# Root mean square norms in a two-layer token mixer: scaled squares, one vector step ahead of the root, and half of the gating beside it

## The chip, the cores and the metric

The kernel runs on one core of a Trainium2 chip. The metric is the device time of one execution in microseconds, the median over several runs. The engines are named as in the profile: PE is TensorE (PEld is its weight load), DVE is VectorE, ACT is ScalarE, POOL is GpSimd and SP is SyncE, which issues most transfers.

## The reference

Two layers, 256 latent and 256 context tokens of width 1024. In each layer the tokens go through a mixer (one wide projection, a two-way RG-LRU branch and a two-way HGRN2 branch, both projected, gated and merged) and through a convolutional SwiGLU FFN. What the change touches are the norms around them:

```python
def rms_norm(x, g):
    x32 = x.astype(jnp.float32)
    y = x32 * lax.rsqrt(jnp.mean(x32 * x32, axis=-1, keepdims=True) + EPS)
    return (y * g.astype(jnp.float32)).astype(x.dtype)
...
        hl = rms_norm(xl, g_pre_mix[l]) * (1.0 + ml[1]) + ml[0]
...
        xl = xl + ml[2] * rms_norm(yl, g_post_mix[l])
        hl = rms_norm(xl, g_pre_ffn[l]) * (1.0 + ml[4]) + ml[3]
```

A mixer or FFN output is normalised, multiplied by a gate row (which holds the post-norm's gain too) and added to the stream; the stream is normalised again, scaled and shifted for the next projection.

## The kernel before

All products run on PE in 32-bit floats, split in two: an operand x becomes a high part (a rounding copy on ACT, `whi` at L236 for weights) and a low part (a subtraction on DVE, `wlo` at L237), and `mm3` issues three matmuls for one product (L242 to L244). Weights come in pieces of one megabyte (`raw`), each cut into two pieces of 128x1024; in the first pieces behind a stage boundary (`self.fine`) a piece is cut into four quarters of 128x256. Feature products (`feat_group`) hold weights as the stationary side and move 512 tokens in layer 0 and 256 in most of layer 1; so layer 1 and a few groups of layer 0 consist of 256-column matmuls.

The output projections (`tok_product`, L495) put tokens on partitions: two rows of 128 tokens, each in two PSUM banks of 512 columns. `post` (L465) takes them over, row by row. ACT squares each half and accumulates its sum (L473, two columns of `ss`). DVE multiplies each half with the gate row (`yg`, L474). `rstd` (L399) adds the two sums (L402), then calls `rpow` (L405), which scales by 1/width and adds EPS (L408) and has POOL raise the result to -1/2 (L410). DVE adds `yg` times the root to the stream row `xt` (L477), in two halves. If a norm follows, `norm_row` (L414) squares `xt` on ACT (L419), takes its root by the same `rstd`, and scales it on DVE into `xh` (L422). After both rows, `norm_cols` (L430) transposes `xh` on PE (L436), applies scale and shift on ACT (L441) and DVE (L443), and forms the low part (L445); these tiles are the moving side of the next products.

`post` runs six times: layer-0 mixer for context and latent, layer-0 FFN for both, layer-1 mixer and layer-1 FFN for the latent tokens; the last one has no norm behind it and writes the output. `norm_rows` does four more rows at the start. So `rstd` runs 12 + 10 + 4 = 26 times; `rpow` is also called 16 times by the HGRN2 heads (L975).

The order of each engine's instructions is settled at compile time by a scheduler that goes by priority and by its own estimate of when operands are ready; `post` runs under `high_priority`. So weight subtractions for the next stage can stand between the steps of a norm on DVE. An order edge without a semaphore (`add_manual_dep` with NoSync) fixes which of two instructions on one engine comes first. `act` (L92) uses it to keep the activations with tables in program order. Small tiles come from the pool `sm`, four buffers for each tag; `rstd` uses the tag `ms` and `rpow` the tags `m1` and `r1` for one column.

Of the kernel before, what the change touches and what calls it, by code (L numbers as in the profile page):

```python
# [8 lines left out]
F32 = mybir.dt.float32  # L9
F32R = mybir.dt.float32r  # L10
U8 = mybir.dt.int32
AF = mybir.ActivationFunctionType
ALU = mybir.AluOpType

P = 128
D = 1024
# [5 lines left out]
EPS = 1e-6  # L22
# [29 lines left out]
class Net:  # L52
# [36 lines left out]
        return self.ax.tile([P, 512], F32, tag="ax", name=self.nm("ax"))  # L89


    def act(self, **kw):  # L92
        ins = self.nc.scalar.activation(**kw)  # L93
        if self.last is not None:
            self.tc.add_manual_dep(ins.ins if hasattr(ins, "ins") else ins, self.last, mybir.DependencyInfo(
                mybir.DependencyClass.NoSync, mybir.DependencyReason.DATA), reason="table order")
        self.last = (ins.ins if hasattr(ins, "ins") else ins).name
        return ins


# [295 lines left out]
                            for j in range(4)])  # L396


    def rstd(self, ss, width):  # L399
        nc = self.nc  # L400
        ms = self.sm.tile([P, 1], F32, tag="ms", name=self.nm("ms"))
        nc.vector.tensor_tensor(out=ms, in0=ss[:, 0:1], in1=ss[:, 1:2], op=ALU.add)  # L402
        return self.rpow(ms, 1, width)

    def rpow(self, ss, n, width):  # L405
        nc = self.nc
# [7 lines left out]
    def norm_row(self, xt, x):  # L414
        nc = self.nc
        ss = self.sm.tile([P, 2], F32, tag="ss2", name=self.nm("ss"))
        halves = [slice(0, 512), slice(512, D)]
        for j, sl in enumerate(halves):
            nc.scalar.activation(out=x[:, sl], in_=xt[:, sl], func=AF.Square, accum_out=ss[:, j:j + 1])  # L419
        rs = self.rstd(ss, D)  # L420
        for sl in halves:
            nc.vector.tensor_scalar(out=x[:, sl], in0=xt[:, sl], scalar1=rs, scalar2=None, op0=ALU.mult)  # L422

# [41 lines left out]
    def post(self, pool, pss, st, gate, xts, xdst, norm=None):  # L465
        nc = self.nc
        xh = [pool.tile([P, D], F32, tag="xh", name=self.nm("xh"), bufs=2) for _ in xts]
        cols = [slice(0, 512), slice(512, D)]
        for i, (halves, xt, x) in enumerate(zip(pss, xts, xh)):
            ss = self.sm.tile([P, 2], F32, tag="ss2", name=self.nm("ss"))  # L470
            yg = pool.tile([P, D], F32, tag="yg", name=self.nm("yg"), bufs=2)
            for j, (ps, sl) in enumerate(zip(halves, cols)):
                nc.scalar.activation(out=x[:, sl], in_=ps, func=AF.Square, accum_out=ss[:, j:j + 1])  # L473
                nc.vector.tensor_tensor(out=yg[:, sl], in0=ps, in1=gate[:, sl], op=ALU.mult)  # L474
            rs = self.rstd(ss, D)
            for sl in cols:
                nc.vector.scalar_tensor_tensor(out=xt[:, sl], in0=yg[:, sl], scalar=rs, in1=xt[:, sl],  # L477
                                               op0=ALU.mult, op1=ALU.add)
                if not norm:
                    nc.sync.dma_start(out=xdst[2 * st + i][:, sl], in_=xt[:, sl])  # L480
            if norm:
                nc.sync.dma_start(out=xdst[2 * st + i], in_=xt)
                self.norm_row(xt, x)
        if norm:
            a, s, h, psum = norm
            for k2 in range(KD // 2):
                self.norm_cols(pool, xh, a, s, st, h, k2, psum)
# [7 lines left out]
    def tok_product(self, w, nk, act, psum):  # L495
        nc = self.nc
        pss = [[psum() for _ in range(2)] for _ in range(2)]
        pcs = {}

        def step(i, k):  # L500
            hi, lo = pcs[k]
            ah, al = act(k, i)
            for n in range(2):
                out = pss[i][n]
                nc.tensor.matmul(out=out, lhsT=ah, rhs=hi[:, n, :], start=k == 0, stop=False)  # L505
                nc.tensor.matmul(out=out, lhsT=ah, rhs=lo[:, n, :], start=False, stop=False)  # L506
            for n in range(2):
                nc.tensor.matmul(out=pss[i][n], lhsT=al, rhs=hi[:, n, :], start=False, stop=k == nk - 1)  # L508

        for k0 in range(0, nk, 2):  # L510
            raw = self.raw()
            r3 = raw.rearrange("p (k n) -> p k n", k=2)
            nc.sync.dma_start(out=r3, in_=w[k0 * P:(k0 + 2) * P, :].rearrange("(k p) n -> p k n", p=P))
            for kk in range(2):
                pcs[k0 + kk] = self.piece(r3[:, kk, :].rearrange("p (a b) -> p a b", a=2), (2, 512))
            ks = [k for k in (k0, k0 + 1) if k < nk - 3]
            for i in range(2):
                for k in ks:
                    step(i, k)
        for i in range(2):  # L520
            for k in range(nk - 3, nk):
                step(i, k)
        return pss
# [750 lines left out]
```

## Time and profile before

| | us |
|---|---|
| median of three runs | 1762.72 |
| lowest, highest run | 1760.85, 1768.89 |
| the profiled execution | 1772.73 |
| its span, first to last instruction | 1771.0 |

The profile is of one execution. Its page gives the busy time of each engine over the span; lists by line give count and duration of each kind of instruction; the timeline gives single instructions with the idle time of the engine ahead of them in brackets, and who ended it. A mean over the whole span says little of the norms, since they run in six short stages; these are read from the timeline and from windows.

### The profile page before, as it was taken

Reading aid. Unit: us, or ns where it says so; the run is one execution under the profiler, and the core shown is the slowest. Engines: PE = TensorE matmul, PEld = TensorE weight load, DVE = VectorE, ACT = ScalarE, POOL = GpSimd, SP = SyncE. Lnnn points to the kernel's source line nnn. Section 1 sums busy time; section 2 is a strip of 40 time slices with the busy share of each in tenths; the row PEclk is TensorE's granted clock in tenths of the full one; section 3 lists DMA queues with packets and bytes.
Section 4 is the critical chain, followed back from the end, with each engine's and each line's share of the span. In section 5 each row is a group of like instructions: output and inputs, shape, how many; then the busy total and the mean of one; then the engine's idle time right before and its main releaser. Section 6 shows DMA issues by size and latency. Waiting matters only on the chain.

```text
span 1771.0 us, 30585 instructions
## 1 busy us (share of the span) xinstructions
PE 1695.1 (96%) x12279; PEld 1421.9 (80%) x12279; DVE 1271.5 (72%) x2313; ACT 903.4 (51%) x1567; POOL 39.9 (2%) x65
## 2 busy tenths in 40 slices
PE   6999999999999999999999999999989999979998
PEld 3777887888888877878878877788987778979996
DVE  3688777788687787987676476777558776767754
ACT  3886823344443446533333355887435554555543
POOL 1000000000000000000000000000000000000000
PEclk9999999999999999999999999999999999989999
DMA  9422377333333376455454674333773424555563
GB/s 295 133 84 84 113 224 230 121 117 100 97 122 99 124 250 257 137 189 170 148 188 143 198 260 165 104 109 109 240 238 115 135 85 132 199 169 182 183 221 119
DMA packets 235289, 282.91 MB, mean 160 GB/s; under 512 B 18156, under 2 KB 211324, under 8 KB 235148
## 3 DMA queue, kind: packets, MB, share of 16 engines
q1 hardware_dynamic: 232156, 271.35, 46.7%
q10 hardware_dynamic: 2880, 9.51, 1.5%
q8 instruction: 96, 1.57, 0.4%
q14 instruction: 45, 0.37, 0.1%
q0 software_dynamic: 112, 0.11, 0.0%
HBM read 263.09 MB, written 17.85 MB: 159 GB/s over the span
## 4 chain that ended last, share of the span: by engine, by line
PE 66%; DVE 16%; DMA 7%; ACT 7%; issue 3%; POOL 1%; SPq 1%; DVEq 0%; POOLq 0%; ACTq 0%
PE mm L242 15%; PE mm L243 15%; PE mm L244 15%; DVE wlo L237 4%; PE mm L506 3%; PE mm L505 3%; PE mm L508 3%; DVE acc L307 2%; DMA raw<-in_w_ada_dram 2%; ACT whi L236 2%; DMA dm<-sb 1%; PE ax L850 1%; ACT r L93 1%; PE ax L506 1%; PE ax L508 1%
## 5 line engine op out<-in xcount | busy, mean ns | idle before, releaser
L242 PE MATMUL mm<-hi,whi 128*128 128x512 f32 (+1 forms) x1792 | 621.4, 348 | 3.6 <-DVE sb L697 2.3
L243 PE MATMUL mm<-lo,whi 128*128 128x512 f32 (+1 forms) x1792 | 618.6, 345 | 4.9 <-DVE lo L445 4.8
L244 PE MATMUL mm<-hi,wlo 128*128 128x512 f32 (+1 forms) x1792 | 616.4, 344 | 2.0 <-DVE wlo L237 1.9
L237 DVE TENSOR_TENSOR wlo<-raw,whi 128x1024 fp32r<-128x1024 f32 (+1 forms) x408 | 436.3, 1080 | 250.8 <-ACT whi L236 237.6
L236 ACT ACTIVATE whi<-raw 128x1024 fp32r<-128x1024 f32 (+1 forms) x408 | 378.6, 943 | 435.6 <-PE mm L243 229.3
L242 PEld LDWEIGHTS mm<-hi,whi 128*128 128x128 f32 x1792 | 339.5, 190 | 50.2 <-issue 4.3
L243 PEld LDWEIGHTS mm<-lo,whi 128*128 128x128 f32 x1792 | 339.0, 189 | 46.3 <-DVE lo L445 6.2
L244 PEld LDWEIGHTS mm<-hi,wlo 128*128 128x128 f32 x1792 | 338.2, 189 | 42.9 <-DVE wlo L237 3.2
L307 DVE SCALAR_TENSOR_TENSOR acc<-raw,s,acc 128x256 f32<-128x256 f32 x448 | 194.4, 478 | 2.6
L865 DVE TENSOR_TENSOR QK<-QK,T 128x512 f32<-128x512 f32 (+1 forms) x84 | 101.5, 1219 | 8.5 <-PE ax L850 5.2
L242 PE MATMUL mm<-whi,hi 128*128 128x256 f32 x256 | 72.9, 285 | 1.0 <-ACT whi L236 0.9
L243 PE MATMUL mm<-wlo,hi 128*128 128x256 f32 x256 | 72.1, 282 | 1.5 <-DVE wlo L237 1.5
L244 PE MATMUL mm<-whi,lo 128*128 128x256 f32 x256 | 71.9, 281 | 0.0
L874 ACT ACTIVATE kt<-QK 128x256 f32<-128x256 f32 (+1 forms) x60 | 40.8, 689 | 58.3 <-DVE QK L865 35.8
L505 PE MATMUL mm<-whi,fh 128*128 128x512 f32 x176 | 68.6, 390 | 0.0
L506 PE MATMUL mm<-wlo,fh 128*128 128x512 f32 x176 | 68.5, 389 | 0.0
L410 POOL TENSOR_TENSOR rs<-ms,mhalf 128x1 f32<-128x1 f32 (+2 forms) x42 | 29.7, 706 | 1549.3 <-DVE ms L408 1549.3
L93 ACT ACTIVATE acc<-acc 128x512 f32<-128x512 f32 (+1 forms) x44 | 22.6, 516 | 69.1 <-DVE acc L1081 64.3
L508 PE MATMUL mm<-whi,fl 128*128 128x512 f32 x176 | 54.2, 389 | 0.0
L242 PEld LDWEIGHTS mm<-whi,hi 128*128 128x128 f32 x256 | 48.9, 191 | 2.9 <-ACT whi L236 1.1
L243 PEld LDWEIGHTS mm<-wlo,hi 128*128 128x128 f32 x256 | 49.0, 191 | 2.2 <-DVE wlo L237 2.2
L244 PEld LDWEIGHTS mm<-whi,lo 128*128 128x128 f32 x256 | 48.9, 191 | 0.0
(225 smaller groups left out, 2466.2 us busy)
## 6 DMA issues: line engine op xcount, KB each, us to landing
raw<-in_w_in_dram SPq DMA_DIRECT2D x72, 1024.0 KB
raw<-in_w_ada_dram SPq DMA_DIRECT2D x48, 1024.0 KB
raw<-in_ffn_w_up_dram SPq DMA_DIRECT2D x44, 1024.0 KB
raw<-in_ffn_w_down_dram SPq DMA_DIRECT2D x33, 1024.0 KB
raw<-in_w_out_dram SPq DMA_DIRECT2D x12, 1024.0 KB
raw<-in_w_proj_rg_dram SPq DMA_DIRECT2D x8, 1024.0 KB
raw<-in_w_proj_hg_dram SPq DMA_DIRECT2D x8, 1024.0 KB
xs<-xt SPq DMA_DIRECT2D x10, 512.0 KB
```

Source lines behind the costliest of these rows:

```text
L93: ins = self.nc.scalar.activation(**kw)
L236: nc.scalar.activation(out=v(hi)[:, part, :], in_=src[:, part, :], func=AF.Copy)
L237: nc.vector.tensor_tensor(out=v(lo)[:, part, :], in0=src[:, part, :], in1=v(hi)[:, part, :], op=ALU.subtract)
L242: nc.tensor.matmul(out=out, lhsT=L[0], rhs=R[0], start=start, stop=False)
L243: nc.tensor.matmul(out=out, lhsT=L[0], rhs=R[1], start=False, stop=False)
L244: nc.tensor.matmul(out=out, lhsT=L[1], rhs=R[0], start=False, stop=stop)
L307: nc.vector.scalar_tensor_tensor(out=acc[:, st, :], in0=r3[:, k, :], scalar=s, in1=acc[:, st, :], op0=ALU.mult, op1=ALU.add)
L505: nc.tensor.matmul(out=out, lhsT=ah, rhs=hi[:, n, :], start=k == 0, stop=False)
L506: nc.tensor.matmul(out=out, lhsT=ah, rhs=lo[:, n, :], start=False, stop=False)
L508: nc.tensor.matmul(out=pss[i][n], lhsT=al, rhs=hi[:, n, :], start=False, stop=k == nk - 1)
L865: nc.vector.tensor_tensor(out=u, in0=u, in1=sub(t, 1, [[-1, 2], [2, W2 // B], [0, B]]), op=ALU.mult)
L874: nc.scalar.activation(out=kt.rearrange("p (n h j) -> p n h j", h=2, j=B), in_=sub(qk, W2, [[2 * B, W2 // (2 * B)], [W2 + B, 2], [1, B]]), ...
```

## The change

The squares carry a scale of 1/sqrt(1024) (`ROOT`), so that the accumulated sums of the two halves are means already. `rstd` then takes one DVE step, which adds the two columns and EPS, in place of the addition and the scale-and-add, and calls POOL itself; the buffer tag `m1` is no longer used. In `post` the gate product of the second half is put behind that step by an order edge, so that DVE does it while POOL takes the root. The helper `behind` makes the edge, and `act` now uses it too, with the same effect as before.

```diff
+    def behind(self, ins, first):
+        self.tc.add_manual_dep(getattr(ins, "ins", ins), getattr(first, "ins", first).name, mybir.DependencyInfo(
+            mybir.DependencyClass.NoSync, mybir.DependencyReason.DATA), reason="order")
...
         if self.last is not None:
-            self.tc.add_manual_dep(ins.ins if hasattr(ins, "ins") else ins, self.last, mybir.DependencyInfo(
-                mybir.DependencyClass.NoSync, mybir.DependencyReason.DATA), reason="table order")
-        self.last = (ins.ins if hasattr(ins, "ins") else ins).name
+            self.behind(ins, self.last)
+        self.last = ins
...
-    def rstd(self, ss, width):
+    def rstd(self, ss):
         nc = self.nc
         ms = self.sm.tile([P, 1], F32, tag="ms", name=self.nm("ms"))
-        nc.vector.tensor_tensor(out=ms, in0=ss[:, 0:1], in1=ss[:, 1:2], op=ALU.add)
-        return self.rpow(ms, 1, width)
+        first = nc.vector.tensor_scalar(out=ms, in0=ss[:, 0:1], scalar1=ss[:, 1:2], scalar2=EPS, op0=ALU.add, op1=ALU.add)
+        rs = self.sm.tile([P, 1], F32, tag="r1", name=self.nm("rs"))
+        nc.gpsimd.tensor_tensor(out=rs, in0=ms, in1=self.mhalf[:, 0:1], op=ALU.pow)
+        return rs, first
+
+
+    ROOT = D ** -0.5
...
-            nc.scalar.activation(out=x[:, sl], in_=xt[:, sl], func=AF.Square, accum_out=ss[:, j:j + 1])
-        rs = self.rstd(ss, D)
+            nc.scalar.activation(out=x[:, sl], in_=xt[:, sl], func=AF.Square, scale=self.ROOT, accum_out=ss[:, j:j + 1])
+        rs, _ = self.rstd(ss)
...
             for j, (ps, sl) in enumerate(zip(halves, cols)):
-                nc.scalar.activation(out=x[:, sl], in_=ps, func=AF.Square, accum_out=ss[:, j:j + 1])
-                nc.vector.tensor_tensor(out=yg[:, sl], in0=ps, in1=gate[:, sl], op=ALU.mult)
-            rs = self.rstd(ss, D)
+                nc.scalar.activation(out=x[:, sl], in_=ps, func=AF.Square, scale=self.ROOT, accum_out=ss[:, j:j + 1])
+            nc.vector.tensor_tensor(out=yg[:, cols[0]], in0=halves[0], in1=gate[:, cols[0]], op=ALU.mult)
+            rs, first = self.rstd(ss)
+
+            self.behind(nc.vector.tensor_tensor(out=yg[:, cols[1]], in0=halves[1], in1=gate[:, cols[1]], op=ALU.mult), first)
```

## Rows read from the trace of the kernel before

**Rows 1.** The page, first part: busy us (share of the span) and instructions.

```profile
PE 1695.1 (96%) x12279; PEld 1421.9 (80%) x12279; DVE 1271.5 (72%) x2313; ACT 903.4 (51%) x1567; POOL 39.9 (2%) x65
```

**Rows 2.** Lists of L402, L408, L410: count, ns min/median/max, first and last start.

```profile
L402 DVE TENSOR_TENSOR ms<-ss x26: 144/151/160, 7.4 to 1765.0; 128x1 f32<-128x1 f32 x26
...
L408 DVE TENSOR_SCALAR ms<-ms x26: 139/148/155, 7.6 to 1765.2; 128x1 f32<-128x1 f32 x26
...
L410 POOL TENSOR_TENSOR rs<-ms,mhalf x42: 548/596/1394, 7.9 to 1765.5; 128x1 f32<-128x1 f32 x26, 128x4 f32<-128x4 f32 x8, 128x2 f32<-128x2 f32 x8
```

**Rows 3.** Timeline of PE in the post-norm stages: start, us, engine, line [idle <-releaser].

```profile
691.39 1.53 PE L436 MATMUL mm<-ident,xh 128*128 128x128 f32 x12 [0.58 <-DVE xh L422]
...
713.55 0.38 PE L244 MATMUL mm<-hi,wlo 128*128 128x256 f32 x1 [1.40 <-DVE wlo L237]
...
1048.25 1.53 PE L436 MATMUL mm<-ident,xh 128*128 128x128 f32 x12 [0.57 <-DVE xh L422]
...
1096.20 1.53 PE L436 MATMUL ax<-ident,xh 128*128 128x128 f32 x12 [1.51 <-DVE xh L422]
...
1567.31 1.05 PE L436 MATMUL ax<-ident,xh 128*128 128x128 f32 x4 [3.83 <-DVE xh L422]
1572.89 2.82 PE L436 MATMUL ax<-ident,xh 128*128 128x128 f32 x12 [4.53 <-DVE xh L422]
```

**Rows 4.** Timeline of the tail, behind the last matmul.

```profile
1763.84 1.29 DVE L474 TENSOR_TENSOR yg<-mm,gt 128x512 f32<-128x512 f32 x2 [0.39 <-ACT xh L473]
1764.19 0.20 ACT L473 ACTIVATION_READ_ACCUMULATOR xh<-mm 128x1 f32 x1
1765.05 0.15 DVE L402 TENSOR_TENSOR ms<-ss 128x1 f32<-128x1 f32 x1
1765.23 0.15 DVE L408 TENSOR_SCALAR ms<-ms 128x1 f32<-128x1 f32 x1
1765.53 0.55 POOL L410 TENSOR_TENSOR rs<-ms,mhalf 128x1 f32<-128x1 f32 x1 [3.53 <-DVE ms L408]
```

**Rows 5.** List by line and shape, Sigmoid with scale -1 and without: us, mean ns.

```profile
L93 ACT ACTIVATE QK<-mm 128x512 f32<-128x512 f32 x16 | 9.6, 600 | 0.0
...
L93 ACT ACTIVATE T<-mm 128x512 f32<-128x512 f32 x16 | 9.5, 596 | 0.0
```

**Rows 6.** Timeline of DVE, layer-1 mixer: two pairs of the norm's steps.

```profile
1565.46 0.15 DVE L402 TENSOR_TENSOR ms<-ss 128x1 f32<-128x1 f32 x1
...
1565.86 0.15 DVE L408 TENSOR_SCALAR ms<-ms 128x1 f32<-128x1 f32 x1
...
1567.48 0.15 DVE L402 TENSOR_TENSOR ms<-ss 128x1 f32<-128x1 f32 x1
...
1567.88 0.14 DVE L408 TENSOR_SCALAR ms<-ms 128x1 f32<-128x1 f32 x1
```

**Rows 7.** Timeline, layer-0 FFN, context: a power and a weight subtraction.

```profile
1042.30 1.21 DVE L237 TENSOR_TENSOR wlo<-raw,whi 128x1024 fp32r<-128x1024 f32 x1
...
1042.52 1.39 POOL L410 TENSOR_TENSOR rs<-ms,mhalf 128x1 f32<-128x1 f32 x1 [2.93 <-DVE ms L408]
```

**Rows 8.** Timeline, layer-0 mixer, context: a power and a gate half.

```profile
683.10 0.68 DVE L474 TENSOR_TENSOR yg<-mm,gt 128x512 f32<-128x512 f32 x1
...
683.27 0.56 POOL L410 TENSOR_TENSOR rs<-ms,mhalf 128x1 f32<-128x1 f32 x1 [4.53 <-DVE ms L408]
```

**Rows 9.** Windows: PE, PEld, DVE, ACT, POOL busy, granted clock, DMA share, GB/s.

```profile
1563.00:1568.00 5.00, 1.17 (x7) 0.56 (x5) 4.93 (x16) 4.32 (x14) 0.56 (x1) 0.96 0.26 105
...
1576.00:1581.00 5.00, 4.42 (x21) 4.13 (x21) 4.86 (x10) 2.07 (x5) 0.00 (x0) 0.50 0.00 0
```

**Rows 10.** Windows of PE alone (256-column matmuls only): busy (count), clock, DMA, GB/s.

```profile
1255.00:1302.00 47.00, 47.00 (x417) 1.00 0.73 236
...
sum 128.00, PE 128.00; mean PE 14.22
...
1591.00:1703.00 112.00, 112.00 (x953) 1.00 0.58 188
```

## The prediction, made before the result was known

> **What bounds the kernel now.** I read the page's busy shares first: PE is busy for 1695.1 of 1771.0 us [rows 1], so TensorE sets the time, and a norm counts only where PE waits for it. Three lists by line then show how often the touched steps run: 26 additions of two half sums, 26 scale-and-add steps (L408 has 16 more in the HGRN2 heads, which stay), 26 powers on POOL among 42, each step near 0.15 us on DVE and the power near 0.6 us [rows 2]. Next I listed PE's waits in the stages where a post-norm runs; the reader is to see the bracket at the end of each row, the idle time and who ended it. Six waits end on the norm chain or on DVE work queued behind it [rows 3]: 0.58 us (layer-0 mixer, context), 1.40 (layer-0 mixer, latent), 0.57 (layer-0 FFN, context), 1.51 (layer-0 FFN, latent), and 3.83 and 4.53 (layer-1 mixer, where PE has nothing else to do). With the tail after the last matmul, where the chain alone runs [rows 4], that is the whole field: 12.4 us of waits and some 4 us of tail. The four norms at the start of the program wait beside PE's own wait for a weight transfer, so I cost them at nothing; the transfer is the cover.
>
> **The change part by part.**
>
> *Scale in Square.* The instruction count stays; a scale rides in the same ACTIVATE. The nearest rows are Sigmoid with and without a scale, 600 and 596 ns for 128x512 [rows 5]. I take 0; the ends are 0 and +4 ns for each of 52 squares, at most 0.2 us.
>
> *One step in place of two.* The new step adds two columns and a constant on 128x1. No row has this form; the neighbours are 0.151 and 0.148 us at the median [rows 2], so I take 0.15. What goes is one step with its distance. With nothing between, the two start 0.18 us apart [rows 4]. Where the compile-time order has put a quarter of a weight subtraction between them, 0.40 us apart [rows 6]; the second pair there stands for a third like it, 3.6 us later. The subtraction itself is not saved, only the power's wait for it.
>
> *Second gate half under the power.* Where both halves run back to back ahead of the sums, they take 1.29 us together [rows 4]; the second half then leaves the path. In the tail: the last squares' accumulator read starts at 1764.19 and takes 0.20, so it ends at 1764.39; the first gate half ends at about 1764.49 (1763.84 + 1.29/2), so the single step can start at about 1764.5. The power starts 0.30 us after its step now (1765.23 to 1765.53), so at 1764.8 in place of 1765.53: **0.73 us** gained. The ends are 0.55 (0.18 of it left hidden under a late accumulator) and 0.83 (1.29/2 + 0.18).
>
> *The added wait.* The second gate half now stands behind the new step, which waits for ACT's second accumulator. Behind it in DVE's queue stand weight subtractions for the next stage and the residual step. In the tail the accumulator is ready 0.1 us before DVE is, so the wait costs nothing; where ACT is late, DVE loses at most the half that it cannot start, 0.65 us. In the second row of the other stages the gate half already runs beside a power, so only the shorter pair is left to gain.
>
> *Power beside DVE work.* One power took 1.39 us, started 0.22 us into a whole weight subtraction [rows 7]; one beside a gate half took 0.56 [rows 8]. I take 0.56 for the new overlap. The Trainium skill, "SBUF — State Buffer", Who interferes with whom, says that a VectorE instruction with two SBUF inputs blocks a GpSimd instruction that reads SBUF until it is done. The subtraction has two SBUF inputs and the gate half one (the other is PSUM), so the page and both rows agree; its rule speaks against this change only if the gate half counted. Then the power would end about 0.4 us behind the half, as it does behind the subtraction (1042.30 + 1.21 to 1042.52 + 1.39), and the tail's gain would be about 0.43 us.
>
> *The stages with waits.* Layer-1 mixer: three pairs on the chain. In the first, DVE is almost full (4.93 of 5 us [rows 9]), so removing one step gives about 0.1; the other two give 0.4 each, less 0.1 where a subtraction holds the power up. The first row's gate half, 0.65, leaves the path to its residual and to the next squares. Sum 0.1 + 2 x 0.3 + 0.65, some 1.3 us; the low end 0.7 is without that last term, the high end 2.8 lets the order of ACT and DVE close up fully. Layer-0 FFN, latent: the same pattern against a wait of 1.51, so 1.2 (0.4 to 1.5). Layer-0 mixer, latent: there a subtraction stood behind the residual step that waited for the power, so the wait of 1.40 may shrink: 0.8 (0 to 1.4). The two context stages: the last pair is 0.2 apart and the waits are 0.58 and 0.57: 0.4 together (0 to 1.15).
>
> *The clock.* PE restarts after the layer-1 mixer at a granted clock of 0.50, its level of 1.2 GHz, having been busy for 1.17 us only between 1563 and 1568 [rows 9]. PE still idles for several us there, so I count no change; the ends are a restart that is fully fast, a gain of some 2.2 us (half of the 4.42 us for which PE is busy at that level between 1576 and 1581), and no change.
>
> *Sum.* 0.73 + 1.3 + 1.2 + 0.8 + 0.4 = 4.4 us, between 1.7 and 7.7 without the clock. The profiled execution took 1772.73 us (span 1771.0, 1.73 around it) and would take 1768.3. It stands 10 us over the median of the three runs, 1762.72; I take the same 4.4 us off that: **1758.3 us**.
>
> **The rivals.** *A, PE restarts at the quicker pace.* Windows in which PE does nothing but 256-column matmuls at full clock show two paces: 417 in 47 us, 112.7 ns each, and 953 in 112 us, 117.5 ns each [rows 10]. The slow stretch begins with the restart after the layer-1 mixer and holds through the layer-1 FFN, while other stretches hold the quick pace. What sets the pace is not shown; it changes only at interruptions, so a restart moved by a microsecond may fall the other way. Price: 953 x 4.8 ns = 4.6 us, so 1753.7 us. *B, little of it is on the path.* DVE's order could keep subtractions between the step and the power, or ACT could be what ends last, so that beyond the tail only half a microsecond remains: 1.2 us gained, 1761.5 us. The full DVE in [rows 9] speaks for it, the waits in [rows 3] against. Here too belongs that the order edge does nothing: in second rows the gate half is already under a power. *C, slower.* The quick stretches, 128 us in nine windows [rows 10], fall to the slow pace: each of the 1140 or so matmuls (128/0.1127) costs 4.8 ns more, 5.5 us. It could come from the moved restarts, or from memory: the tag for the second step's four buffers is gone, so every tile allocated behind it moves. Since the gain is 4.4 us, C decides from about 920 matmuls on. With the sum at its low end of 1.7 us the time is 1762.7 - 1.7 + 5.5 = 1766.5 us; were the wide matmuls moved too, it could be more, and nothing in the trace prices that. For C: the paces do differ. Against: quick stretches appear after many different interruptions.
>
> **How the numbers follow.** Chances: the forecast 0.46, A 0.24, B 0.16, C 0.14. The forecast's own range is 1755.0 to 1761.0 (the sum between 1.7 and 7.7). The range that should hold it 8 times in 10 runs from 1750 (A with the sum at its high end: 1762.7 - 7.7 - 4.6) to 1767 (C). A measurement of this kernel can tell about 0.5%, 8.8 us, from no change: under 1753.9 is faster, over 1771.5 slower. Faster: somewhat over half of A, 0.14, and of the forecast the end with the clock's gain, 0.11: 0.25. Slower: half of C, 0.07, and 0.02 for mishaps in the order: 0.09. The same: 0.66.
>
> **What would show it.** Right: 26 single steps near 0.15 us and no L402 pair; in the tail, the power starting 0.7 us sooner after the squares, 0.56 us long, with the second gate half beside it; the waits of 3.83 and 4.53 us shorter by about 1.3 together; 1.51, 1.40 and 0.37 shorter. Wrong: powers of 1 us and more in the post-norms; PE's waits unchanged, with subtractions between step and power; a layer-1 FFN at 112.7 ns for each narrow matmul (A), or quick stretches at 117.5 (C).

## The result, and the profile after

The changed kernel took 1775.76 us (median of six runs, 1773.09 to 1779.67) beside 1765.81 us for the kernel before (six runs, 1759.3 to 1769.25): a ratio of 1.0067, 95% interval 1.0044 to 1.0090. By the ratio it is slower by some 12 us (the two medians stand 10 us apart), where 4.4 us less had been forecast, and it lies outside the forecast's range of 1755.0 to 1761.0 and the wider one that ended at 1767. The profiled execution took 1775.03 us. Its mean granted clock was 0.995, beside 0.991 in the profiled execution of the kernel before, so a lower clock is not what made it slower.

The first line of the page after answers to [rows 1]: PE is busy for 1705.4 us in place of 1695.1, with the same 12279 matmuls, while DVE has 26 instructions fewer, as planned.

```profile
span 1773.3 us, 30552 instructions
...
PE 1705.4 (96%) x12279; PEld 1419.6 (80%) x12279; DVE 1270.7 (72%) x2287; ACT 903.2 (51%) x1567; POOL 38.9 (2%) x65
```

So the added time is busy time of an engine that the change does not touch. The list of PE by line and shape says which matmuls: first the kernel before, then the one after (columns: shapes, count | busy us, mean ns | idle before).

```profile
L242 PE MATMUL mm<-hi,whi 128*128 128x512 f32 x992 | 395.2, 400 | 3.3 <-DVE sb L697 2.3 <-ACT whi L236 0.9
L243 PE MATMUL mm<-lo,whi 128*128 128x512 f32 x992 | 392.6, 396 | 1.6 <-DVE lo L445 1.6
L244 PE MATMUL mm<-hi,wlo 128*128 128x512 f32 x992 | 391.5, 395 | 0.5 <-DVE wlo L237 0.5
...
L505 PE MATMUL mm<-whi,fh 128*128 128x512 f32 x176 | 68.6, 390 | 0.0
```

```profile
L246 PE MATMUL mm<-hi,whi 128*128 128x512 f32 x992 | 399.5, 404 | 3.0 <-DVE sb L708 2.5 <-ACT whi L240 0.5
L247 PE MATMUL mm<-lo,whi 128*128 128x512 f32 x992 | 396.8, 400 | 1.5 <-DVE lo L454 1.5
L248 PE MATMUL mm<-hi,wlo 128*128 128x512 f32 x992 | 396.4, 400 | 0.0
...
L516 PE MATMUL mm<-whi,fh 128*128 128x512 f32 x176 | 68.6, 390 | 0.0
```

The reader is to see two things. The wide (512-column) feature products became 4, 4 and 5 ns longer on the mean, which is 992 x 13 ns = 12.9 us; the token products, of the same size and just as many columns (L505 before, L516 after), did not. Windows in which PE does nothing but one kind of wide product say the same as a pace. In each kernel the first window holds feature products of layer 0, the second token products of the layer-0 FFN, the third the 256-column products of the layer-1 FFN (columns: window, its length, PE busy and count, granted clock, DMA share, GB/s; the third window of before stands in [rows 10]).

Before:

```profile
177.00:237.00 60.00, 60.00 (x266) 1.00 0.45 148
963.00:1033.00 70.00, 70.00 (x311) 1.00 0.60 201
```

After:

```profile
177.00:237.00 60.00, 60.00 (x260) 1.00 0.45 151
973.00:1043.00 70.00, 70.00 (x310) 1.00 0.59 203
1591.00:1703.00 112.00, 111.98 (x986) 1.00 0.59 191
```

At the same granted clock, 60 us hold 266 feature products before and 260 after: 225.6 against 230.8 ns each. The token products keep their 225 ns (70 us / 311). The 256-column products of the layer-1 FFN even ran at the quicker of their two paces (986 in 112 us beside 953), the outcome that rival A had priced at 4.6 us, and it did not save the kernel. Elsewhere the narrow products lost: all nine quick stretches of [rows 10] are slower, as rival C had it. Windows of the same lengths, 128 us in all, hold 1107 products after where they held 1149, and the longest, 417 in 47 us before, holds 402:

```profile
1264.00:1311.00 47.00, 47.00 (x402) 1.00 0.73 237
```

What separates the two kinds of wide product is where their operands lie in SBUF. The addresses are those of the compiled programs; no view of the profile shows them. Tag `m1`, which the change drops, held four buffers of 32 bytes per partition. All tiles of the left side that are allocated behind it start 128 bytes earlier now; the weight tiles, which stand ahead of it, and the tiles of the token products' activations (`mh`, `fh`, right side) stay. Taken mod 256, that is as the remainder after division by 256 bytes, the start of the moving tile of a feature product (`hi`, `lo`, `xg`, `yh`) was 128 before and is 0 after. Its weights start at 128 in both; the token products have 128 on both sides in both kernels.

**Theories.** *T1*: the move of the tiles in memory slows the wide feature products and buries the gain of the norms; as *T1a* it is the distance between the two operands' starts that counts, as *T1b* the moving tile's own address. *T2*: the new order and timing of the norms (a step that took longer, other restarts of PE) makes the time, and the place does not matter.

### The profile page after: what moved, and what is told of

It reads as the page before. It is cut to its first block, busy times and chain, and to the rows that moved or that the text cites. A ratio compares the mean times of both kernels' runs of the same rounds, so it can differ in the third digit from the quotient of the medians.

```text
span 1773.3 us, 30552 instructions
## 1 busy us (share of the span) xinstructions
PE 1705.4 (96%) x12279; PEld 1419.6 (80%) x12279; DVE 1270.7 (72%) x2287; ACT 903.2 (51%) x1567; POOL 38.9 (2%) x65
## 4 chain that ended last, share of the span: by engine, by line
PE 73%; DVE 13%; ACT 5%; DMA 5%; issue 2%; POOL 1%; SPq 1%; DVEq 0%; POOLq 0%; ACTq 0%
PE mm L246 18%; PE mm L247 18%; PE mm L248 17%; DVE wlo L241 3%; PE mm L517 3%; PE mm L516 3%; PE mm L519 3%; DMA raw<-in_w_ada_dram 1%; DVE acc L311 1%; PE ax L861 1%; ACT whi L240 1%; PE ax L517 1%; PE ax L519 1%; PE ax L516 1%; DMA raw<-in_w_out_dram 1%
## 5 line engine op out<-in xcount | busy, mean ns | idle before, releaser
L241 DVE TENSOR_TENSOR wlo<-raw,whi 128x1024 fp32r<-128x1024 f32 (+1 forms) x408 | 435.6, 1080 | 263.7 <-ACT whi L240 250.4
L516 PE MATMUL mm<-whi,fh 128*128 128x512 f32 x176 | 68.6, 390 | 0.0
```

The source lines that it names most:

```text
L241: nc.vector.tensor_tensor(out=v(lo)[:, part, :], in0=src[:, part, :], in1=v(hi)[:, part, :], op=ALU.subtract)
```

## The experiments

Times are medians; ratios are to the kernel before on the same chip. The first four kernels shared 29 runs of before (1765.84 us), the next four 23 (1764.63), the last four one (1763.35).

**1. The changed kernel, its tiles put back.**

```diff
-FILL = (24, 16, 24)
+FILL = (24, 48, 24)
```

The second number is the size of a filler tile in the pool `sm`, in floats: 32 floats more are the missing 128 bytes.

> The changed kernel with 128 bytes of filler put where the dropped tag m1 stood, so that every tile allocated behind it lies where it lay before the change; all instructions stay those of the changed kernel. T1 (the move of the tiles in memory costs about 9 to 14 us and hides a gain from the norms): 4 us under the kernel before, ratio 0.9975 (0.995 to 0.999), and the wide feature matmuls fall back to some 395 ns mean from 400 to 404. T2 (the new order and timing of the norms costs the time, the place in memory does not matter): as the changed kernel, ratio 1.006 to 1.007.

Measured: 1762.80 us, ratio 0.9982 (0.9962 to 1.0002), 13.0 us under the changed kernel's median, with all of its instructions kept. The means of the feature products are 400, 397 and 395 ns again, and the window of the feature products has 266:

```profile
span 1762.9 us, 30552 instructions
...
PE 1690.3 (96%) x12279; PEld 1417.4 (80%) x12279; DVE 1270.7 (72%) x2287; ACT 903.6 (51%) x1567; POOL 39.1 (2%) x65
```

```profile
177.00:237.00 60.00, 60.00 (x266) 1.00 0.45 146
```

T2 is out: all of the change's instructions and order edges are still there, and the loss is gone.

**2. The kernel before, its tiles shifted.** The second step writes in place, so that `m1` goes; steps, order and gating stay those of before.

```diff
-        ms = self.sm.tile([P, n], F32, tag=f"m{n}", name=self.nm("ms"))
+        ms = ss if n == 1 else self.sm.tile([P, n], F32, tag=f"m{n}", name=self.nm("ms"))
```

> The kernel before with the scale-and-add step of the norms written in place, so that tag m1 goes and every tile behind it moves by 128 bytes as in the changed kernel; both steps, the order and the gate halves stay those of before. T1 (place in memory): slower than the kernel before by 9 to 14 us, ratio 1.005 to 1.008, with the wide feature matmuls at 400 to 404 ns mean. T2 (order and timing): ratio 1.000 (0.998 to 1.002), wide matmuls at 395 ns.

Measured: 1777.61 us, ratio 1.0063 (1.0042 to 1.0084). The whole loss of the change, without the change:

```profile
L242 PE MATMUL mm<-hi,whi 128*128 128x512 f32 x992 | 398.7, 403 | 3.3 <-DVE sb L697 2.8 <-ACT whi L236 0.6
L243 PE MATMUL mm<-lo,whi 128*128 128x512 f32 x992 | 396.1, 399 | 1.5 <-DVE lo L445 1.5
L244 PE MATMUL mm<-hi,wlo 128*128 128x512 f32 x992 | 395.4, 399 | 0.0
```

```profile
177.00:237.00 60.00, 60.00 (x260) 1.00 0.51 172
```

**3. The changed kernel, its weights moved after the tiles.** The slices of `whi` and `wlo` start 128 bytes further on (mod 256).

```diff
+        at = (line + 2) % 4
-        hi = pool.tile([P, 1088], F32R, tag="whi", ...)[:, 16 * line:16 * line + 1024]
+        hi = pool.tile([P, 1088], F32R, tag="whi", ...)[:, 16 * at:16 * at + 1024]
```

(and `lo` alike; `line`, 0 for wide and 1 for narrow feature products, was there before: it moves the slice by 64 bytes a step.)

> The changed kernel with the slices of its weight tiles whi and wlo taken 128 bytes further on (mod 256), all else as in the changed kernel. T1a (the wide matmuls are slow where the moving tile's start and the weights' start stand in a certain relation mod 256): the feature products that had slowed come back to a start-to-start interval of 226 to 227 ns, and the token products, whose moving tiles lie at 384 mod 512, slow to 229 to 232; total within 5 us of the kernel before. T1b (the moving tile's own address decides): feature products stay at 229 to 232 ns, token products stay at 226 to 227, ratio 1.005 to 1.008. T2 (order and timing): no change, ratio 1.006 to 1.007.

Measured: 1764.65 us, ratio 1.0002 (0.9982 to 1.0022). The feature products are quick again at an address at which they had been slow, and the token products, whose weights now stand 128 bytes from their activations, are slow, by the windows as by their means:

```profile
173.00:233.00 60.00, 60.00 (x266) 1.00 0.45 149
963.00:1033.00 70.00, 70.00 (x302) 1.00 0.58 196
```

```profile
L517 PE MATMUL mm<-whi,fh 128*128 128x512 f32 x176 | 69.8, 397 | 0.0
L518 PE MATMUL mm<-wlo,fh 128*128 128x512 f32 x176 | 69.2, 393 | 0.0
```

That is T1a: the distance decides, and T1b is out.

**4. Tiles put back, one step only.** As the first, but with both gate halves ahead of the step again.

```diff
-            nc.vector.tensor_tensor(out=yg[:, cols[0]], in0=halves[0], in1=gate[:, cols[0]], op=ALU.mult)
+                nc.vector.tensor_tensor(out=yg[:, sl], in0=ps, in1=gate[:, sl], op=ALU.mult)
...
-            self.behind(nc.vector.tensor_tensor(out=yg[:, cols[1]], in0=halves[1], in1=gate[:, cols[1]], op=ALU.mult), first)
```

> The changed kernel with the tiles back at their places of before (128 bytes of filler) and with the gate halves both ahead of the step again, so that of the change only the scale in the squares and the single step are left. T1: the single step alone is worth 0.18 us in the tail and some 1 to 2 us in all, so 1 to 3 us over the first kernel of this call and 1 to 3 us under the kernel before, ratio 0.998 to 1.000. T2, if the gate half in its new place is what costs: about the kernel before, while the first kernel stays at 1.006; T2, if the single step costs: 1.006 here too.

Measured: 1762.15 us, ratio 0.9985 (0.9968 to 1.0001). That the first kernel would be 1 to 3 us quicker than this one does not show: the totals cannot tell the gate half's share. The timeline can (below, in the tail and in the layer-1 mixer).

**5. The kernel before, its weights moved.** The edit of 3 on the kernel before, so that every wide product of both kinds, but for the gates' own, has its operands 128 bytes apart.

> The kernel before, untouched but for the slices of its weight tiles, taken 128 bytes further on (mod 256), so that no wide product has its moving tile and its weights at the same place mod 256. T1a (equal starts mod 256 are quick, starts 128 apart are slow): feature products slow by the 9.8 us of start-to-start intervals that the changed kernel shows against the first kernel of the first call, token products by the 5.1 us that the third kernel shows; together 15 us, ratio 1.0085 (1.006 to 1.011), wide feature matmuls at 400 to 404 ns mean and the 176 token matmuls of one line at 395 to 397 in place of 390. T1b (the moving tile's own address): the feature products' moving tiles have not moved and stay at 226 to 227 ns, ratio 1.000 to 1.004. T2 (order and timing of the norms): 1.000.

Measured: 1782.45 us, ratio 1.0115 (1.0088 to 1.0142), 17.8 us. It holds T1a, and T1b and T2 fall again. My 15 us were a little low. They came from intervals between starts, which leave out every interval at which another kind of matmul follows; the means of the list would have given 12.9 us for the features and some 5 ns for each of 1080 token products, 18 us. Both windows are slow:

```profile
177.00:237.00 60.00, 60.00 (x259) 1.00 0.52 174
975.00:1045.00 70.00, 70.00 (x303) 1.00 0.66 229
```

**6. Half of the shift.** The changed kernel with 64 bytes of filler more.

```diff
-FILL = (24, 16, 24)
+FILL = (24, 32, 24)
```

> The changed kernel with 64 of the missing 128 bytes put back: the feature products' moving tiles start 64 bytes from their weights mod 256, the token products have equal starts as before. T1a in its strict form (only equal starts are quick): feature products as slow as in the changed kernel, 229 to 232 ns start to start, ratio 1.005 to 1.008. T1a by distance: half the price, ratio 1.000 to 1.003, 228 to 229 ns. If only a distance of 128 bytes is slow: ratio 0.997 to 0.999, 226 to 227 ns. T2: 1.006 to 1.007.

Measured: 1785.30 us, ratio 1.0111 (1.0081 to 1.0140). A distance of 64 bytes is no better for the wide products than 128. The ratio is above the 1.008 of the strict form, which had not counted that the narrow ones lose as well: their operands, 64 apart in the kernel before, are 128 apart here, and in the layer-1 FFN 927 of them run in 110 us (118.7 ns), short of the quick pace.

```profile
177.00:237.00 60.00, 60.00 (x259) 1.00 0.51 169
973.00:1043.00 70.00, 70.00 (x310) 1.00 0.61 208
1603.00:1713.00 110.00, 110.00 (x927) 1.00 0.58 190
```

**7. Narrow products with equal starts.** The first kernel with `line` at 0 for narrow feature products too.

```diff
-        pieces = pieces or self.prep(w, c0, line=int(narrow))
+        pieces = pieces or self.prep(w, c0)
```

> The changed kernel with all tiles back at their places, and the weights of the narrow (256-column) feature products put at the same place mod 256 as their moving tiles, where before they stand 64 bytes on. If the rule of equal starts holds for the narrow products too: nearly all of their 3552 intervals at 113 ns, where the runs so far show between 13 and 69 per cent of them there, so up to 5 us less than the first kernel of the first call, ratio to the kernel before 0.995 to 0.998. If the two narrow paces have nothing to do with place: 0.998, as that kernel. If the 64 bytes are what keeps the narrow products at the quick pace at times: some 3 to 5 us more than it, 1.000 to 1.002.

Measured: 1766.88 us, ratio 1.0016 (0.9997 to 1.0035), about 4 us over the first kernel. The rule of the wide products does not carry over. With equal starts the narrow ones of the layer-1 FFN run at 119.7 ns, 919 in 110 us, and not at the 113 to 114 ns that they have in the first kernel, where 64 bytes lie between:

```profile
1583.00:1693.00 110.00, 110.00 (x919) 1.00 0.56 183
```

**8. The first kernel again.**

> The first kernel of the first call again (the changed kernel with its tiles back at their places), to tell whether it beats the kernel before: there 0.9982, interval 0.9962 to 1.0002. T1: again 0.997 to 0.999, by the 4 us that the norms gain. T2: no expectation of its own is left after the first call.

Measured: 1763.67 us, ratio 0.9998 (0.9977 to 1.0019), above the 0.997 to 0.999 expected. With its tiles in place the change is level with the kernel before: the mean of the two ratios is a gain of 1.8 us, and half the width of either interval is over 3.5 us. By its total no version here beats the kernel before by more than can be told; against the changed kernel as it stood, this one is some 12 us quicker.

The granted clock blurs these totals. Its mean over the executions was 0.9913 in the first experiment and 0.9915 here, beside 0.9929 in the kernel before. Set side by side at equal clock, this kernel's 17 executions at 0.990 to 0.994 took on the mean 4.9 to 8.3 us less than those of the kernel before, level by level (at 0.994, 1754.81 to 1757.02 us beside 1757.58 to 1769.28); its single one at 0.995 took 2.6 us more. This comparison was made afterwards, and why the clock was lower stays open.

**9 to 12. A scan of distances**, one execution each, on the first kernel:

```diff
+        at = {0: w, 1: n, 3: 64 - n}[line]
```

with w, n = 8, 24; 48, 8; 56, 12; 4, 20 floats.

> A scan of places, on the changed kernel with its tiles put back: the weights of the wide products start 32 bytes behind their moving tiles mod 256 (0 so far quick, 64 and 128 slow), those of the narrow products 96 bytes behind (64 so far 113 or 118 ns, 0 only 120). Place rule in its strict form: wide products at 229 to 236 ns start to start, mean 400 or more. Place rule in steps of 64 bytes: wide as at 0, 226 to 227. Narrow: at 113 alone if 96 lies inside the quick stretch, else 117 to 120. If place did not matter: wide 227, narrow 113 and 118 mixed as in the first kernel of the first call.

> The scan goes on: wide weights 192 bytes behind their moving tiles (64 ahead), narrow weights 32 behind. Strict rule for the wide products: 229 to 236 ns, mean 400 or more; a rule that only a start behind the moving tile's is slow: 226 to 227. Narrow: between the 120 of distance 0 and the 113 to 118 of distance 64.

> The scan goes on: wide weights 224 bytes behind (32 ahead), narrow weights 48 behind. Strict rule: wide 229 to 236 ns. Steps of 64 bytes: 226 to 227. Narrow: as at 64 if the rule is gradual, as at 0 if it goes by steps of 64 bytes (120).

> The scan goes on: wide weights 16 bytes behind, narrow weights 80 behind. Strict rule: wide 229 to 236 ns; gradual or in steps of 32 or 64 bytes: 226 to 228. Narrow: as at 64 (113 and 118 mixed) if steps of 64 bytes decide.

Measured: 1783.15, 1783.93, 1784.36 and 1780.18 us, 17 to 21 us over the kernel before. The windows of the narrow products in the layer-1 FFN, one from each kernel in this order:

```profile
1597.00:1707.00 110.00, 110.00 (x928) 1.00 0.58 190
```

```profile
1597.00:1707.00 110.00, 109.99 (x930) 1.00 0.59 192
```

```profile
1597.00:1707.00 110.00, 110.00 (x934) 1.00 0.59 192
```

```profile
1597.00:1707.00 110.00, 110.00 (x928) 1.00 0.58 186
```

None reaches the quick pace (969 in such a window in the first experiment, 968 in the eighth). The window of the wide feature products (177 to 237 us) holds 259 at a distance of 32 bytes, 263 at 192 and 259 at 224, where it holds 266 at 0. At 16 it still holds 267, but over the whole run their means rise to 402, 398 and 397 ns, and the window of the token products (975 to 1045 us), 311 at equal starts, holds 302, so both paces occur there. Of the distances tried, only equal starts mod 256 are quick throughout; the strict rule's forecast for 16 bytes, slow, came true in part.

## Why the prediction was wrong

**The step that failed** is the price of memory in rival C. The text saw that "every tile allocated behind it moves", gave the loss to the narrow products alone (5.5 us), and of the wide ones said that "nothing in the trace prices that"; so the time of C stopped at 1766.5 us, and its chance at 0.14; the forecast's own sum has no term for the move at all. The move cost 13 us (first experiment against the changed kernel) or 11.8 us (second against before), three times the forecast gain. The narrow part of C came about as priced, 42 products fewer in the 128 us of its quick stretches, some 4.9 us (an estimate, at 116 ns each). What the text put at nothing was the larger part: the wide feature products cost 12.9 us by their means. The argument against C, that quick stretches follow many kinds of interruption, speaks of the narrow paces; it says nothing on wide products, which in the kernel before had all their operands at equal starts and so showed no second pace that a trace could have priced. The code gave the hint that the trace could not: slices of the weight tiles shifted by 64 bytes for narrow products, and filler tiles of chosen sizes. The move should have been a term of the sum, with a bound, and not a clause of a rival.

Rival A's pace did come in the profiled execution, at 986 narrow products in 112 us, 33 more than before or some 3.7 us, and about made up for the narrow loss; rival B's 1.2 us and the forecast's 4.4 enclose what the norms gave (3.6 us, below). With these, 12.9 + 4.9 - 3.7 - 3.6 is 10.5 us, an estimate from single profiled executions, beside the 10 to 12 us measured.

Rival A came by the order of the norms, it seems, and not by chance alone. In the layer-1 FFN all four profiled kernels with the second gate half behind the step and narrow distances of 64 or 192 bytes are quick (after, first, third and eighth experiment: 986 in 112 us, 969, 969 and 968 in 110), and all four with both halves ahead of it are slow (before, second, fourth and fifth: 953 in 112 us, 933, 934 and 933 in 110). The first and the fourth experiment differ in the gate half alone:

```profile
1583.00:1693.00 110.00, 109.75 (x969) 1.00 0.60 195
```

```profile
1577.00:1687.00 110.00, 109.97 (x934) 1.00 0.58 191
```

That is one execution of each, and how the order does it is not shown. Nor does the pace change "only at interruptions", as the text of rival A had it: in the kernel before it turns from quick to slow at 1241.9 us without idle time (73 products in the 8 us from 1233, 87 in the 10 us from 1243), where weights stop being the moving operand and become the stationary one.

**The norms themselves** went much as forecast. The timeline of the tail after, against [rows 4]:

```profile
1767.00 0.69 DVE L483 TENSOR_TENSOR yg<-mm,gt 128x512 f32<-128x512 f32 x1 [1.13 <-ACT xh L482]
1767.35 0.20 ACT L482 ACTIVATION_READ_ACCUMULATOR xh<-mm 128x1 f32 x1
1767.61 0.20 DVE L406 TENSOR_SCALAR ms<-ss 128x1 f32<-128x1 f32 x1
1767.73 0.68 DVE L486 TENSOR_TENSOR yg<-mm,gt 128x512 f32<-128x512 f32 x1
1767.96 0.55 POOL L408 TENSOR_TENSOR rs<-ms,mhalf 128x1 f32<-128x1 f32 x1 [3.53 <-DVE ms L406]
```

- *Tail.* From the start of the first gate half to the start of the power it was 1.69 us before (1763.84 to 1765.53) and is 0.96 us after (1767.00 to 1767.96): 0.73 us gained, the number of the forecast, to the hundredth by luck: the step started 0.61 us behind the gate half's start where 0.66 had been reckoned, and the power 0.35 us behind the step in place of 0.30. In the fourth experiment, with one step and the halves together, it is 1.55 us (1752.70 to 1754.25): the step is worth 0.14 and the gate half 0.59.

```profile
1752.70 1.29 DVE L483 TENSOR_TENSOR yg<-mm,gt 128x512 f32<-128x512 f32 x2 [0.53 <-ACT xh L482]
...
1754.25 0.55 POOL L408 TENSOR_TENSOR rs<-ms,mhalf 128x1 f32<-128x1 f32 x1 [3.53 <-DVE ms L406]
```

- *One step in place of two.* It takes 0.205 us at the median, not 0.15. It did no harm, since the distance of the pair that it replaces was larger.

```profile
L406 DVE TENSOR_SCALAR ms<-ss x26: 201/205/215, 7.6 to 1767.6; 128x1 f32<-128x1 f32 x26
```

- *The power beside a gate half.* The row shows 0.55 us, as taken. The Trainium skill, "SBUF — State Buffer", Who interferes with whom, has a VectorE instruction with two SBUF inputs contend with a GpSimd instruction that reads SBUF, because its second input comes through the shared read interface; the gate half has one input in PSUM, and the trace agrees that it does not hold the power up. Over the run, the list of L408 shows that the change also kept the powers clear of the whole (128x1024) subtractions: the longest took 741 ns, beside 1394 in [rows 2] and 1462 with one step only (the second line below, of the fourth experiment).

```profile
L408 POOL TENSOR_TENSOR rs<-ms,mhalf x26: 548/548/741, 7.9 to 1768.0; 128x1 f32<-128x1 f32 x26
```

```profile
L408 POOL TENSOR_TENSOR rs<-ms,mhalf x26: 550/594/1462, 8.2 to 1754.3; 128x1 f32<-128x1 f32 x26
```

- *Layer-1 mixer.* Its waits were 3.83 and 4.53 us [rows 3]; after, the timeline of PE has

```profile
1575.16 0.81 PE L445 MATMUL ax<-ident,xh 128*128 128x128 f32 x4 [2.23 <-DVE xh L431]
...
1580.64 2.82 PE L445 MATMUL ax<-ident,xh 128*128 128x128 f32 x12 [4.68 <-DVE xh L431]
```

  8.36 became 6.91, 1.45 us less; forecast 1.3. With the step alone (fourth experiment) the two were 2.61 and 5.39 us, 8.00 together. So the step gave some 0.4 us and the gate half some 1.1, where the forecast had 0.7 and 0.65: the sum came out, its parts less well.
- *Layer-0 FFN, latent.* Here 1.2 us were forecast and next to nothing came. The wait of 1.51 us [rows 3], and one of 0.20 that [rows 3] lacks, became 0.66 and 0.95 for the two rows' transposes. What those transposes release got no earlier: the waits for `lo` behind them were 1.07 and 1.55 us in the kernel before, and one of 2.17 us stands there after. With a wait of 0.48 us for `wlo`, 4.33 us became 4.26. The prediction priced the first wait of that stage and not what PE waits for next. These are the three rows of before that [rows 3] has not, and two of those after:

```profile
1089.77 0.44 PE L436 MATMUL ax<-ident,xh 128*128 128x128 f32 x2 [0.20 <-DVE xh L422]
...
1100.40 0.39 PE L243 MATMUL mm<-lo,whi 128*128 128x256 f32 x1 [1.07 <-DVE lo L445]
...
1105.64 0.38 PE L243 MATMUL mm<-lo,whi 128*128 128x256 f32 x1 [1.55 <-DVE lo L445]
```

```profile
1103.69 1.53 PE L445 MATMUL ax<-ident,xh 128*128 128x128 f32 x12 [0.95 <-DVE xh L431]
...
1114.31 0.38 PE L247 MATMUL mm<-lo,whi 128*128 128x256 f32 x1 [2.17 <-DVE lo L454]
```

- *Layer-0 mixer, latent, and the contexts.* The wait of 1.40 us for `wlo` and one of 0.37 for transposes, which the prediction names among its signs but counts in no sum, became 0.70 and 0.61 us for transposes: 0.46 gained of 0.8. The first row is of before, the others of after:

```profile
715.90 1.53 PE L436 MATMUL ax<-ident,xh 128*128 128x128 f32 x12 [0.37 <-DVE xh L422]
```

```profile
713.72 0.44 PE L445 MATMUL ax<-ident,xh 128*128 128x128 f32 x2 [0.70 <-DVE xh L431]
719.32 1.53 PE L445 MATMUL ax<-ident,xh 128*128 128x128 f32 x12 [0.61 <-DVE xh L431]
```

  The two context waits, 0.58 and 0.57, became 0.30 and nothing: 0.85 gained of 0.4.
- *Sum.* 0.73 + 1.45 + 0.07 + 0.46 + 0.85 = 3.6 us of 4.4. Where the tiles lie does not enter: each of these waits of the kernel before stands in the second experiment within 0.1 us. PE's idle time, span less busy time from the first lines of the pages, says the same for kernels with tiles in the same place: 75.9 us before against 72.6 in the first experiment; 71.8 in the second (before, shifted) against 67.9 in the changed kernel. That is 3.3 and 3.9 us. The totals, at 0.9982 and 0.9998, are too coarse to show them.

## What to carry to other kernels

A tag that goes, even one of four 32-byte buffers, moves every tile allocated behind it; before a small edit is timed, compare the starts of the large operands with those of the kernel before, and fill the hole, so that the edit alone is measured. Where PE is the bound, the first test of an unexplained change is the pace of one kind of matmul in a gapless window, before and after: if it moved, look at memory before the order. And a wait taken from a chain is worth only what the next wait behind it leaves.

## What the runs showed that was not expected

- In this kernel a 512-column matmul of 32-bit floats runs at 225.6 ns (266 in 60 us) where its two operands start at the same place mod 256 bytes, and at 228 to 232 ns (263 to 259 in 60 us) where they start 32, 64, 128, 192 or 224 bytes apart; at 16 the run shows both. The place itself, at the two places tried, does not matter (third experiment).
- 256-column matmuls follow another rule: in the layer-1 FFN they took 119.7 ns at distance 0, and the quick pace, 113 to 114 ns over a whole window, was seen only at distances 64 and 192 (986 in 112 us after), where 117.5 to 118 ns is seen as well (953 in 112 us at 64 in [rows 10]; 933 in 110 us at 192 in the second experiment). In that stage, at these two distances, the pace went with the place of the gate half in eight executions of eight. In the stretch of [rows 10] that begins at 1255 us it went with the distance: at 64 bytes 417 in 47 us before and in the first, third and fourth experiment, at 192 bytes 402, 402 and 401 in the changed kernel, the second and the fifth. What sets the pace in either stage stays open, and so does the mechanism behind both rules: no run here looks inside the engine's reads.
